# Strassen's form in the second GEMM of both FFN layers, products summed in PSUM in the first, and conditioning work moved to other stages

## The chip, the cores and the metric

One core of a Trainium2 chip runs the whole program in one launch. The metric is the device time of that launch in microseconds; the time before is the median of three runs.

## What is computed

Two layers of a diffusion backbone over 1024 latent tokens and 256 context tokens of width 1024. Layer 0 mixes by a gated convolution and differential attention, layer 1 by pooling and retention. Each layer ends in a gated ConvFFN with a hidden width of 2816, and every sub-layer is modulated by shifts, scales and gates that come from a conditioning vector. The part that matters most here:

```python
def conv_ffn(h, w_up, conv_w, conv_b, w_down):
    a, b = jnp.split(h @ w_up, 2, axis=-1)
    a = dwconv3(a, conv_w) + conv_b
    return (jax.nn.silu(a) * b) @ w_down
```

All of it is float32. The first GEMM is `h @ w_up`, the second is `(...) @ w_down`.

## The kernel before

Activations lie transposed, features on partitions and tokens in two chunks of 512 columns (chunk 0 and chunk 1). A float32 product is made of three matmuls of rounded parts: each operand is split into a high part (a ScalarE cast to fp32r) and a low part, the residual (a subtraction on VectorE or GpSimd); `mm3` (L221) adds high x high, high x low and low x high. `WStream` (L93) loads the weights in a fixed list of units on the SP queue, casts them (L111) and makes the residual (L113), a few units ahead of their use. A tile framework inserts the waits and sets each engine's order of instructions at compile time; the order is static in the program.

**First GEMM of the FFN** (`up_pair`, L867). For 20 of the 22 blocks of 128 hidden features, the pair (a, b) for both token chunks is made in a Strassen-Winograd form: 7 products of 4 x 3 matmuls (`prod`, L792), so 84 matmuls per pair. Each product has a PSUM bank of its own, eight banks in turn (seven in layer 0). The sums of products are made outside: P1 and P5 are copied by ScalarE (L887 or L884, and L894), VectorE adds P6, P2, P7, P4 and P3 (L890, L892, L897, L902, L906), and GpSimd makes two further sums (L898, L899). Then `conv_silu` (L705) does bias and middle tap on ScalarE (L708), two taps on VectorE (L709, L710) and silu on ScalarE (L712); VectorE gates the first half (L907), GpSimd the second (L908), and the block g goes to DRAM (L909). The weight sums of Strassen's form are made in `up_unit` (L771): an add on GpSimd (L783), subtractions on VectorE (L784, L788), and two of the four residuals on GpSimd. Three pairs have their first two products made in advance (`up_pre`, L858).

**Second GEMM**. Layer 0 uses `down` (L912): for each token chunk and each half of the output features, four banks are filled over 22 hidden blocks, 2 x 2 x 22 x 4 x 3 = 1056 matmuls; then VectorE adds the four banks to x (L938). Layer 1 uses `down_fast` (L968): seven products over 11 pairs of hidden blocks, four banks each, 7 x 11 x 4 x 3 = 924 matmuls, chains of products summed in PSUM without a copy, with VectorE adding to x after each of them (L1021). Loads of g and their differences are made three steps ahead.

**Conditioning of layer 1** (`mod_layer1`, L324) is 256 pieces of a matrix-vector product on VectorE (L355), each with a 128 KB load on the SP queue (L338). A row of the conditioning vector is loaded on ScalarE's queue and goes through silu there (L332, L333) whenever the half or the vector changes; one buffer holds it. 120 pieces run beside the first GEMM of layer 0, 136 beside its second GEMM. The results feed the norm ahead of layer 1 and its gates.

**Around it**. `norm` (L382) squares on ScalarE, sums on VectorE, reduces over partitions by matmuls with one column (`colsum`, L370), and spreads the result over partitions by float32 matmuls with the identity (`bcast`, L376). In layer 0 the norms for layer 1 start in the second GEMM: chunk 0 first, at steps 27 and 38, chunk 1 at the end, between the first steps of the token GEMM of layer 1 (`od_tok`, L1049), which takes the token tiles in the order 0 to 9. Behind it come feature GEMM and retention woven together (`retention`, L1227). Both stages have two banks for the GEMM's sums.

Of the kernel before, what the change touches and what calls it, by code (L numbers as in the profile page):

```python
# [9 lines left out]
F32 = mybir.dt.float32  # L10
# [38 lines left out]
XLOAD = ((2, 4, 6, 8, 25, 26, 27, 28), (1, 2, 3, 4, 6, 8, 10, 12))  # L49

DOWN = ((1, 0, 0), (5, 1, 4), (6, 1, 0), (3, 1, 0), (7, 1, 4), (2, 0, 0), (4, 0, 4))
NORM0 = 27


MODA, MODB = 120, (3, 8)
# [81 lines left out]
class Net:  # L137
# [64 lines left out]
    def _lat_units(self, units, L):  # L202
        up, dn = self.I[f"w_up{L}"], self.I[f"w_dn{L}"]
        units.extend([up[f, i] for f in range(PLAIN) for i in range(2)])
        first = range(PLAIN, PLAIN + PRE)
        units.extend([partial(self.up_unit, up, f, 0) for f in first])
        units.extend([partial(self.up_unit, up, f, i, i == 1) for f in first for i in range(1, 4)])
        units.extend([partial(self.up_unit, up, f, i) for f in range(PLAIN + PRE, NF) for i in range(4)])
        if L:
            units.extend([partial(self.down_unit, dn, p, f) for p, _, _ in DOWN for f in range(0, NF // 2, 2)])  # L210
            return
        for _ in range(2):
            for mg in range(2):
                units.extend([dn[f:f + 2, :, mg * 512:(mg + 1) * 512].rearrange("f p m -> p f m")
                              for f in range(0, NF, 2)])
# [26 lines left out]
    def mod_start(self, hp, psA, first):  # L242
# [81 lines left out]
    def mod_layer1(self, row, tile, first, last):  # L324

        nc, I = self.nc, self.I
        todo = [(v, h, mt, j) for v, n in ((1, 16), (0, 48)) for h in range(2) for mt in range(n) for j in range(2)]
# [16 lines left out]
        if last < len(todo):  # L344
            return
        for dst, n in ((self.modC, 48), (self.modD, 16)):
            for q in range(1, 4):
                nc.vector.tensor_tensor(dst[:, :, 0], dst[:, :, 0], dst[:, :, q], op=ALU.add)
            nc.vector.tensor_tensor(dst[:, :, 0], dst[:, :, 0], self.v("modb1", 0, n), op=ALU.add)
        self.gs[(1, 1, 0)] = self.gscale("n1g1", self.modC[:, 8:16, 0])  # L350
        self.gs[(1, 1, 1)] = self.gscale("n1g1", self.modD[:, 8:16, 0])
        self.gs[(1, 2, 0)] = self.gscale("n2g1", self.modC[:, 32:40, 0])
# [418 lines left out]
    def up_unit(self, up, f, i, again=False):  # L771
# [7 lines left out]
        if i == 1:  # L779
# [12 lines left out]
    def prod(self, out, W, half, B):  # L792

        for k in range(4):
            ks = slice((half * 4 + k) * P, (half * 4 + k + 1) * P)
            self.mm3(out, (W[0][:, ks], W[1][:, ks]), (B[k][:, 0, :], B[k][:, 1, :]), k == 0, k == 3)
# [70 lines left out]
    def up_pair(self, L, f, hs, T, big, ps, pre=None):  # L867
        nc = self.nc
        B11, B21, B22 = hs[0][:4], hs[0][4:], hs[1][4:]
        bank = lambda n: ps.tile([P, 512], F32, tag="mm", name=n)  # L870
# [4 lines left out]
        p1, u2, p5, u3 = t2k("p1"), t2k("u2"), u("p5"), u("u3")  # L875

        def product(n, W, half, B):
            pt = bank(n)
            self.prod(pt, W, half, B)
            return pt  # L880
# [31 lines left out]
    def down(self, xk, galloc, ps, gate, done):  # L912

        nc = self.nc
        gs = ([], [])
        loads = [(c * NF + f // 2, c, f + j) for c in range(2) for f in range(0, NF, 2) for j in range(2)]
        for c in range(2):
            for mg in range(2):
                pt = [ps.tile([P, 512], F32, tag="mm", name="pd") for _ in range(4)]
                for f in range(0, NF, 2):  # L920
                    while loads and loads[0][0] <= c * NF + mg * (NF // 2) + f // 2 + GAHEAD:
                        _, c1, j = loads.pop(0)
                        raw = self.tmp.tile([P, 512], F32, tag="t2k", name="gr")
                        nc.sync.dma_start(raw, self.gD[j][:, c1 * 512:(c1 + 1) * 512])
                        gt = galloc(j)
                        nc.scalar.copy(gt[:, 0, :], raw)
                        nc.vector.tensor_tensor(gt[:, 1, :], raw, gt.bitcast(F32)[:, 0, :], op=ALU.subtract)  # L927
                        gs[c1].append(gt)
                    W = self.ws.get()
                    for j in range(2):  # L930
                        for m in range(4):
                            ms = slice(j * 512 + m * P, j * 512 + (m + 1) * P)
                            gt = gs[c][f + j]
                            self.mm3(pt[m], (W[0][:, ms], W[1][:, ms]), (gt[:, 0, :], gt[:, 1, :]), f + j == 0, f + j == NF - 1)
                    yield
                for m in range(4):
                    mm = mg * 4 + m
                    nc.vector.scalar_tensor_tensor(xk[c](mm), in0=pt[m], scalar=gate(mm), in1=xk[c](mm),  # L938
                                                   op0=ALU.mult, op1=ALU.add)
                    done(c, mm)  # L940
# [27 lines left out]
    def down_fast(self, xk, galloc, ps, gate, done):  # L968
# [80 lines left out]
    def od_tok(self, qp, ps, hs):  # L1049
# [177 lines left out]
    def retention(self, rp, ps, feat):  # L1227
# [25 lines left out]
        for item in range(17):  # L1253
# [22 lines left out]
            fill(RFILL[2 + item])  # L1276
        for _ in range(3):
# [42 lines left out]
    def rest(self, stop=99):  # L1320
# [20 lines left out]
        def tail(L, xin, xmid, src, gate1, gs, sh, gate2, done, step=lambda phase, i, alloc: None):  # L1341

            with ExitStack() as s:
# [4 lines left out]
                ps = Pool(pF, {t: ("mm", 8) for t in ("mm", "tp", "st")} if L else {"mm": ("mm", 7), "tp": ("n", 1), "st": ("n", 1)})  # L1348
# [42 lines left out]
                s6f = lambda: s6().bitcast(F32)[:, 0, :]  # L1391
                alloc = (s6f, lambda: s6f()[:, :256])
                galloc, work = (lambda j: s4() if j < 14 else s5()), self.down
                if L:
                    self.dalloc = lambda: p4.tile([P, 1024], F32, tag="s4", name="s4f")
                    self.dS = {}
                    turn = [0]

                    def galloc():
                        turn[0] += 1  # L1400
                        return s6() if turn[0] % 3 == 0 else s5()

                    work = self.down_fast
                for i, _ in enumerate(work(xk, galloc, ps, gate2, lambda c, m: done(c, m, xk, ps))):
                    if i in XLOAD[L]:
                        next(loads[XLOAD[L].index(i) // 4])
                    step(1, i, alloc)
# [5 lines left out]
        def done0(c, m, xk, ps):  # L1413
            nc.sync.dma_start(self.xD[1][c, :, m, :], xk[c](m))
            if m == 7:
# [3 lines left out]
                next(nm[c])  # L1419
# [3 lines left out]
        def step0(phase, i, alloc):  # L1423
            if i == 0:
                mods.append(self.mod_layer1(*alloc, phase * MODA, 256 if phase else MODA))
            if phase == 0:
                pace(mods[0], i, 7 * (NF - PLAIN), MODA + 1)
            else:
                for _ in range(MODB[0] if i < NF // 2 else MODB[1]):
                    next(mods[1], None)  # L1430
            if phase == 1 and i in (NORM0, 38):
# [6 lines left out]
        with ExitStack() as s:  # L1438
            pG = s.enter_context(tc.tile_pool(name="psG", bufs=1, space=PSUM, reuse_waits="tile"))
            ps = Pool(pG, {"mm": ("mm", 2), "at": ("at", 2), "o": ("o", 2), "rst": ("rst", 2), "tp": ("rst", 2), "st": ("rst", 2)})  # L1440
            with ExitStack() as s2:
# [14 lines left out]
                for es in xs:  # L1456
                    es.close()
                next(tok)
                drain(nm[2])
                drain(tok)  # L1460
            with ExitStack() as s2:
                rp = s2.enter_context(tc.tile_pool(name="rp", bufs=1, reuse_waits="tile"))
                rr = Pool(rp, {t: (t, 2) for t in ("am", "qd", "ry", "rsq", "sg", "M", "QD", "V", "kd", "q", "St", "kT")})
                self.retention(rr, ps, self.od_feat(rp, ps, hs))
# [224 lines left out]
```

## Time and profile before

| | us |
|---|---|
| median of 3 runs (2769.24 to 2776.75) | 2772.87 |
| the profiled execution's own time | 2781.38 |
| its span, first to last instruction | 2779.6 |
| first GEMM, layer 0 / layer 1 | 409.0 / 383.5 |
| second GEMM, layer 0 / layer 1 | 286.5 / 209.5 |
| token GEMM of layer 1 | 110.5 |
| feature GEMM and retention | 185.0 |

The mean granted clock of TensorE over the span is 0.966, where 1 is 2.4 GHz and 0.5 is 1.2 GHz. The stages were cut where the tile that TensorE writes changes: P in the first GEMM, pd in the second, pt in the token GEMM, pf in the feature GEMM. In rows of groups, "x" is a number of instructions and idle time is that just before them, with what ended it. A matmul's listed duration is longer than the distance to the next one, since they overlap in the array.

### The profile page before, as it was taken

How to read it: one execution, taken by the hardware profiler on the slowest of the kernel's cores; microseconds unless marked ns; L12 is line 12 of the kernel's file. 1: busy time of each engine (PE TensorE's matmuls, PEld its weight loads, DVE VectorE, ACT ScalarE, POOL GpSimd, SP SyncE). 2: the span in 40 equal slices, each digit the busy share in tenths (PEclk: the TensorE clock that was granted, in tenths of full speed). 3: DMA queues.
4: the chain of work that ended last, by engine and by line, in shares of the span. 5: the costliest groups of instructions: out<-in, count | busy, mean ns of one | idle time of the engine just before them, and what ended most of it. 6: DMA issues, size and time to landing. Idle time of an engine off the chain costs nothing. (4 is left out here: it accounts for less than half of the span.)

```text
span 2779.6 us, 35344 instructions
## 1 busy us (share of the span) xinstructions
PE 2625.0 (94%) x12924; PEld 2206.8 (79%) x12924; DVE 1910.8 (69%) x2815; ACT 1098.5 (40%) x1635; POOL 800.5 (29%) x674
## 2 busy tenths in 40 slices
PE   7999998999898999999998989999999999999999
PEld 6877787888888787787886767787778888888887
DVE  7467856999887577777776665613356767766895
ACT  5322224666665344333333323323234333334342
POOL 3221113444342034444440000102212555544000
PEclk7999998999998999999999999999999999999999
DMA  6224625443322723333338774337363222224874
GB/s 246 93 93 144 197 96 164 127 131 109 109 89 79 245 84 121 114 124 121 123 105 272 246 224 153 121 112 223 115 235 114 76 84 90 85 91 152 286 231 165
DMA packets 203007, 402.26 MB, mean 145 GB/s; under 512 B 19536, under 2 KB 88784, under 8 KB 202448
## 3 DMA queue, kind: packets, MB, share of 16 engines
q1 hardware_dynamic: 199952, 394.87, 43.2%
q10 hardware_dynamic: 2880, 5.12, 0.6%
q8 instruction: 102, 1.67, 0.3%
q14 instruction: 73, 0.60, 0.1%
HBM read 330.19 MB, written 69.73 MB: 144 GB/s over the span
## 5 line engine op out<-in xcount | busy, mean ns | idle before, releaser
L225 PE MATMUL P<-s,wl 128*128 128x512 f32 x1120 | 440.4, 393 | 10.5 <-DVE wl L113 10.2
L223 PE MATMUL P<-s,wh 128*128 128x512 f32 x1120 | 438.9, 392 | 7.8 <-ACT p L884 4.5
L224 PE MATMUL P<-s,wh 128*128 128x512 f32 x1120 | 438.4, 391 | 0.0
L111 ACT CAST wh<-wr 128x1024 fp32r<-128x1024 f32 (+1 forms) x268 | 278.4, 1040 | 392.7 <-DMA wr<-in_w_dn 83.8
L113 DVE TENSOR_TENSOR wl<-wr,wh 128x1024 fp32r<-128x1024 f32 (+1 forms) x231 | 289.3, 1255 | 183.8 <-ACT wh L111 176.3
L223 PE MATMUL pd<-s,wh 128*128 128x512 f32 x660 | 263.2, 399 | 24.9 <-DVE x L938 16.3
L225 PE MATMUL pd<-s,wl 128*128 128x512 f32 x660 | 261.8, 397 | 2.5 <-DVE wl L113 2.5
L224 PE MATMUL pd<-s,wh 128*128 128x512 f32 x660 | 262.2, 397 | 0.6 <-DVE s L927 0.6
L225 PEld LDWEIGHTS P<-s,wl 128*128 128x128 f32 x1120 | 211.8, 189 | 59.2 <-DVE wl L113 15.5
L223 PEld LDWEIGHTS P<-s,wh 128*128 128x128 f32 x1120 | 212.1, 189 | 53.9 <-ACT p L884 5.4
L224 PEld LDWEIGHTS P<-s,wh 128*128 128x128 f32 x1120 | 211.9, 189 | 44.6
L363 POOL TENSOR_TENSOR rr<-vv,mhalf 128x8 f32<-128x8 f32 (+2 forms) x39 | 56.6, 1451 | 520.1 <-DVE vv L361 520.1
L223 PEld LDWEIGHTS pd<-s,wh 128*128 128x128 f32 x660 | 127.1, 193 | 54.3 <-DVE x L938 17.6
L225 PEld LDWEIGHTS pd<-s,wl 128*128 128x128 f32 x660 | 126.8, 192 | 30.7 <-DVE wl L113 4.1
L224 PEld LDWEIGHTS pd<-s,wh 128*128 128x128 f32 x660 | 127.1, 193 | 28.4 <-DVE s L927 1.5
L113 POOL TENSOR_TENSOR wl<-s,wh 128x1024 fp32r<-128x1024 f32 x40 | 101.6, 2540 | 148.0 <-ACT wh L111 148.0
L709 DVE SCALAR_TENSOR_TENSOR fcv<-a,vec,fcv 128x1024 f32<-128x1024 f32 (+1 forms) x66 | 71.1, 1078 | 102.6 <-ACT fcv L708 102.6
L111 ACT CAST wh<-r 128x1024 fp32r<-128x1024 f32 x80 | 67.1, 839 | 178.7 <-DVE r L784 99.7
L708 ACT ACTIVATE fcv<-a,vec 128x1024 f32<-128x1024 f32 (+1 forms) x66 | 68.5, 1037 | 174.5 <-POOL a L899 166.4
L113 POOL TENSOR_TENSOR wl<-wr,wh 128x1024 fp32r<-128x1024 f32 x37 | 94.3, 2550 | 134.0 <-ACT wh L111 125.5
L1511 ACT ACTIVATE p<-S,s 128x1280 f32<-128x1280 f32 (+1 forms) x80 | 92.6, 1158 | 69.5 <-DVE s L1509 65.4
L783 POOL TENSOR_TENSOR r<-r 128x512 f32<-128x512 f32 x40 | 72.5, 1813 | 132.1 <-DMA r<-in_w_up 100.9
(373 smaller groups left out, 6680.2 us busy)
## 6 DMA issues: line engine op xcount, KB each, us to landing
wr<-in_w_dn SPq DMA_DIRECT2D x101, 512.0 KB, 4.5
wr<-in_w_up SPq DMA_DIRECT2D x98, 512.0 KB, 3.6
gr<-gD SPq DMA_DIRECT2D x121, 256.0 KB, 4.0
gD<-fcv SPq DMA_DIRECT2D x44, 512.0 KB, 2.8
wr<-in_w_out SPq DMA_DIRECT2D x40, 512.0 KB, 3.7
r<-in_w_up SPq DMA_DIRECT2D x40, 512.0 KB, 3.3
s<-in_mod1T SPq DMA_DIRECT2D x136, 128.0 KB, 3.5
mbw<-in_mod0T SPq DMA_DIRECT2D x32, 512.0 KB, 3.9
```

The source lines that it names most:

```text
L111: self.nc.scalar.copy(hi, raw)
L113: eng.tensor_tensor(lo, raw, hi.bitcast(F32), op=ALU.subtract)
L223: mm(out, L[0], R[0], start=first, stop=False)
L224: mm(out, L[0], R[1], start=False, stop=False)
L225: self.last_mm = mm(out, L[1], R[0], start=False, stop=last)
L363: self.last_pow = nc.gpsimd.tensor_tensor(r, vv, self.mhalf[:, :n], op=ALU.pow)
L708: nc.scalar.activation(t, a[:, 1:N + 1], AF.Identity, bias=self.v(f"fcb{L}", f), scale=w[1])
L709: nc.vector.scalar_tensor_tensor(t, in0=a[:, 0:N], scalar=w[0], in1=t, op0=ALU.mult, op1=ALU.add)
L783: nc.gpsimd.tensor_tensor(r1[:, 1536:], r1[:, 512:1024], r1[:, :512], op=ALU.add)
L1511: nc.scalar.activation(e, sv, AF.Exp, bias=s2[:, m:m + 1], accum_out=self.s1[:, qt:qt + 1] if m == 0 else s2[:, 2:3])
```

## The change

- Layer 0's second GEMM takes the function of layer 1 (`down_fast`, now named `down`); the plain one goes. All eight banks serve it. Chunk 1 is done first now, so the token GEMM takes tiles 4 to 7 first, and the norm's steps are 67 and 70.
- The first GEMM of both layers sums in PSUM: P1, P6, P7 and P4 in bank A, P5 and P3 in bank B, P2 in bank C; ScalarE copies A after P1, P6 and P4 and B after P5; VectorE makes the other sums.
- GpSimd keeps no arithmetic in the first GEMM's loop: weight sum, two residuals and the second gating go to VectorE.
- Conditioning: 128 pieces beside layer 0's first GEMM, in a new order so that shift and scale are done there; the other 128 in the token GEMM (3 per step) and the retention (5 per item), with three buffers for pieces and one for the row. One buffer instead of two holds the retention's kd.
- `bcast` and the first rows use `transpose` with a broadcast operand instead of a float32 matmul.

```diff
-XLOAD = ((2, 4, 6, 8, 25, 26, 27, 28), (1, 2, 3, 4, 6, 8, 10, 12))
+XLOAD = (1, 2, 3, 4, 6, 8, 10, 12)
+NORM0 = (67, 70)
-NORM0 = 27
-MODA, MODB = 120, (3, 8)
+MODA, MODT, MODR = 128, 3, 5
...
-                    nc.tensor.matmul(rb[:, k * P:(k + 1) * P], self.silc[:, h * 4 + k, v:v + 1].broadcast_to([P, P]), self.ident,
-                                     start=True, stop=True)
+                    nc.tensor.transpose(rb[:, k * P:(k + 1) * P], self.silc[:, h * 4 + k, v:v + 1].broadcast_to([P, P]),
+                                        self.ident)
...
-        todo = [(v, h, mt, j) for v, n in ((1, 16), (0, 48)) for h in range(2) for mt in range(n) for j in range(2)]
+        todo = [(v, h, mt, j) for v, a, b in ((1, 0, 16), (0, 0, 16), (0, 16, 48)) for h in range(2) for mt in range(a, b)
+                for j in range(2)]
...
-                self.nc.tensor.matmul(rb[:, j * P:(j + 1) * P], r[:, j:j + 1].broadcast_to([P, P]), self.ident,
-                                      start=True, stop=True)
+                self.nc.tensor.transpose(rb[:, j * P:(j + 1) * P], r[:, j:j + 1].broadcast_to([P, P]), self.ident)
...
-            nc.gpsimd.tensor_tensor(r1[:, 1536:], r1[:, 512:1024], r1[:, :512], op=ALU.add)
+            nc.vector.tensor_tensor(r1[:, 1536:], r1[:, 512:1024], r1[:, :512], op=ALU.add)
...
-            return ws.split(s34, nc.gpsimd)
-        return ws.split(self.r1[:, :512], nc.gpsimd)
+            return ws.split(s34, nc.vector)
+        return ws.split(self.r1[:, :512], nc.vector)
...
         if pre:
-            nc.scalar.copy(p1, pre[0])
+            A, C = pre
+            nc.scalar.copy(p1, A)
+            yield
         else:
             W0 = self.ws.get()
-            nc.scalar.copy(p1, product("P1", W0, 0, B11))
+            A, C = (ps.tile([P, 512], F32, tag="mm", name=n) for n in ("PA", "PC"))
+            self.prod(A, W0, 0, B11)
+            nc.scalar.copy(p1, A)
+            yield
+            self.prod(C, W0, 1, B21)
+        V(p1, p1, C, op=ALU.add)
         yield
+
         W1 = self.ws.get()
-        V(u2, p1, product("P6", W1, 0, T[2]), op=ALU.add)
+        self.prod(A, W1, 0, T[2], False)
+        nc.scalar.copy(u2, A)
         yield
-        V(p1, p1, pre[1] if pre else product("P2", W0, 1, B21), op=ALU.add)
-        yield
-        nc.scalar.copy(p5, product("P5", W1, 1, T[1]))
+        B = ps.tile([P, 512], F32, tag="mm", name="PB")
+        self.prod(B, W1, 1, T[1])
+        nc.scalar.copy(p5, B)
         yield
         W2 = self.ws.get()
-        V(u3, u2, product("P7", W2, 0, T[3]), op=ALU.add)
-        nc.gpsimd.tensor_tensor(u2, u2, p5, op=ALU.add)
-        nc.gpsimd.tensor_tensor(a[:, 513:1025], u3, p5, op=ALU.add)
+        self.prod(A, W2, 0, T[3], False)
+        V(a[:, 513:1025], p5, A, op=ALU.add)
+        yield
+        self.prod(B, W2, 1, B22, False)
+        V(u2, u2, B, op=ALU.add)
         yield
         W3 = self.ws.get()
-        V(a[:, 1:513], u3, product("P4", W3, 0, T[4]), op=ALU.add)
-        yield
-        P3 = product("P3", W2, 1, B22)
+        self.prod(A, W3, 0, T[4], False)
+        nc.scalar.copy(a[:, 1:513], A)
         self.conv_silu(L, f, a, t, SEQ)
-        V(u2, u2, P3, op=ALU.add)
         V(t[:, :512], t[:, :512], p1, op=ALU.mult)
-        nc.gpsimd.tensor_tensor(t[:, 512:], t[:, 512:], u2, op=ALU.mult)
+        V(t[:, 512:], t[:, 512:], u2, op=ALU.mult)
...
-            for tt in range(10):
+            for tt in (4, 5, 6, 7, 0, 1, 2, 3, 8, 9):
...
             fill(RFILL[2 + item])
+            for _ in range(MODR):
+                next(mod, None)
+        drain(mod)
...
+                mp = s.enter_context(tc.tile_pool(name="mp", bufs=1, side="right", reuse_waits="tile"))
+                mods.append(self.mod_layer1(lambda: mp.tile([P, 512], F32, tag="cr2", name="cr2"),
+                                            lambda: mp.tile([P, 256], F32, tag="mw2", name="mw2", bufs=3), MODA, 256))
                 next(tok)
                 drain(nm[2])
-                drain(tok)
+                for _ in tok:
+                    for _ in range(MODT):
+                        next(mods[1], None)
```

## Rows read from the trace of the kernel before

**Rows 1.** The page, busy time (us, share of the span), instructions of an engine

```profile
PE 2625.0 (94%) x12924; PEld 2206.8 (79%) x12924; DVE 1910.8 (69%) x2815; ACT 1098.5 (40%) x1635; POOL 800.5 (29%) x674
```

**Rows 2.** Busy time by stage; columns in the first row; stages in order of time

```profile
core 0: us, PE busy (x) PEld busy (x) DVE busy (x) ACT busy (x) POOL busy (x), PEclk, DMA share, GB/s
1054.00:1463.00 409.00, 392.62 (x1682) 319.10 (x1680) 305.07 (x487) 140.73 (x168) 196.89 (x163) 0.98 0.37 122
1463.00:1749.50 286.50, 257.57 (x1074) 208.16 (x1073) 170.75 (x415) 93.88 (x121) 11.39 (x8) 0.94 0.70 221
1749.50:1860.00 110.50, 108.91 (x503) 89.47 (x504) 48.07 (x85) 32.13 (x55) 9.91 (x12) 1.00 0.31 105
1860.00:2045.00 185.00, 175.42 (x811) 138.47 (x810) 68.91 (x106) 57.67 (x79) 48.78 (x50) 0.96 0.53 165
2182.50:2566.00 383.50, 381.64 (x1683) 315.35 (x1682) 256.13 (x247) 144.84 (x171) 197.18 (x163) 1.00 0.29 99
2566.00:2775.50 209.50, 209.50 (x925) 173.12 (x923) 163.29 (x213) 82.09 (x114) 1.79 (x1) 1.00 0.68 229
```

**Rows 3.** The same view, instructions of tile pd alone (PE, PEld, DVE), both second GEMMs

```profile
1463.00:1749.50 286.50, 256.14 (x1056) 206.16 (x1056) 11.13 (x16) 0.94 0.70 221
2566.00:2775.50 209.50, 209.50 (x924) 173.12 (x923) 18.20 (x27) 1.00 0.68 229
```

**Rows 4.** Waits of PE in 1463 to 1750: us in total, times, longest

```profile
PE pd L223 <- DVE x L938: 16.3, 3, 7.5
```

**Rows 5.** Busy time by stage, 15 us that begin as the longest of these waits ends

```profile
1613.00:1628.00 15.00, 14.35 (x55) 11.75 (x56) 11.59 (x30) 5.32 (x8) 0.00 (x0) 0.85 0.78 260
```

**Rows 6.** Timeline of PE: start us, us, what (bcast at 2111, transposes at 1818)

```profile
2111.50 1.05 PE L379 MATMUL rb<-ident,rr 128*128 128x128 f32 x8
2112.31 0.48 PE L223 MATMUL po<-s,wh 128*128 128x512 f32 x1
...
1818.20 0.60 PE L548 MATMUL tpq<-ident,m 128*128 128x128 f32 x4
1818.56 0.48 PE L223 MATMUL pt<-wh,s 128*128 128x512 f32 x1
```

**Rows 7.** Waits of PE in 1054 to 1463, the first GEMM of layer 0

```profile
PE P L225 <- DVE wl L113: 8.6, 9, 3.5
PE P L223 <- ACT p L884: 4.3, 1, 4.3
PE P L223 <- DVE fcv L820: 2.1, 1, 2.1
```

**Rows 8.** Groups of VectorE in 2182.5 to 2566, layer 1's first GEMM: busy us, mean ns

```profile
L113 DVE TENSOR_TENSOR wl<-r,wh 128x1024 fp32r<-128x1024 f32 x20 | 44.2, 2209 | 0.0
L784 DVE TENSOR_TENSOR r<-r,wr 128x512 f32<-128x512 f32 x20 | 28.7, 1434 | 40.6 <-POOL r L783 40.6
L113 DVE TENSOR_TENSOR wl<-wr,wh 128x1024 fp32r<-128x1024 f32 x21 | 25.6, 1219 | 0.5 <-PE P L225 0.3 <-ACT wh L111 0.2
...
L902 DVE TENSOR_TENSOR a<-u,P 128x512 f32<-128x512 f32 x19 | 13.1, 689 | 15.4 <-PE P L225 14.2
```

**Rows 9.** Timeline of ACT, one turn from pair to pair, layer 1's first GEMM

```profile
2304.16 1.25 ACT L708 ACTIVATE fcv<-a,vec 128x1024 f32<-128x1024 f32 x1 [5.90 <-POOL a L899]
...
2308.55 1.06 ACT L712 ACTIVATE fcv<-fcv 128x1024 f32<-128x1024 f32 x1 [2.20 <-DVE fcv L710]
2309.52 0.57 ACT L887 COPY p<-P 128x512 f32<-128x512 f32 x1
```

**Rows 10.** Timeline of ACT, the second row of conditioning in layer 0's first GEMM

```profile
1167.82 0.34 ACTq L332 DMA_DIRECT2D cr<-in_crow  x1
1170.40 0.63 ACT L333 ACTIVATE cr<-cr 128x512 f32<-128x512 f32 x1 [6.59 <-DMA cr<-in_crow]
```

**Rows 11.** Pieces of conditioning by tile and by line L355: duration ns min/median/max

```profile
L338 SPq DMA_DIRECT2D mw<-in_mod1T x120: 327/382/1908, 1076.0 to 1461.0; - x120
...
L355 DVE SCALAR_TENSOR_TENSOR s<-s,s x136: 410/425/1520, 1475.8 to 1691.6; 128x256 f32<-128x256 f32 x136
```

More of the change, by code (lines that the diff above doesn't have):

```diff
@@ L208, in _lat_units @@
         units.extend([partial(self.up_unit, up, f, i) for f in range(PLAIN + PRE, NF) for i in range(4)])
[L209 to L215, printed above, removed]
+        units.extend([partial(self.down_unit, dn, p, f) for p, _, _ in DOWN for f in range(0, NF // 2, 2)])
     def v(self, name, i=0, n=1):
@@ L343, in mod_layer1 @@
             self.mod_piece(*d)
-        if last < len(todo):
-            return
-        for dst, n in ((self.modC, 48), (self.modD, 16)):
+        early = last == MODA
+        for dst, a, b in ((self.modC, 0, 16), (self.modD, 0, 16)) if early else ((self.modC, 16, 48),):
             for q in range(1, 4):
[L348 to L352, printed above, removed]
+                nc.vector.tensor_tensor(dst[:, a:b, 0], dst[:, a:b, 0], dst[:, a:b, q], op=ALU.add)
+            nc.vector.tensor_tensor(dst[:, a:b, 0], dst[:, a:b, 0], self.v("modb1", a, b - a), op=ALU.add)
+        if early:
+            self.gs[(1, 1, 0)] = self.gscale("n1g1", self.modC[:, 8:16, 0])
+            self.gs[(1, 1, 1)] = self.gscale("n1g1", self.modD[:, 8:16, 0])
+        else:
+            self.gs[(1, 2, 0)] = self.gscale("n2g1", self.modC[:, 32:40, 0])
     def mod_piece(self, w, c, d):
@@ L788, in up_unit, with prod @@
             nc.vector.tensor_tensor(s34, self.r0, self.r1[:, 512:1536], op=ALU.subtract)
-            return ws.split(s34, nc.gpsimd)
-        return ws.split(self.r1[:, :512], nc.gpsimd)
-    def prod(self, out, W, half, B):
+            return ws.split(s34, nc.vector)
+        return ws.split(self.r1[:, :512], nc.vector)
+    def prod(self, out, W, half, B, new=True):
         for k in range(4):
             ks = slice((half * 4 + k) * P, (half * 4 + k + 1) * P)
-            self.mm3(out, (W[0][:, ks], W[1][:, ks]), (B[k][:, 0, :], B[k][:, 1, :]), k == 0, k == 3)
+            self.mm3(out, (W[0][:, ks], W[1][:, ks]), (B[k][:, 0, :], B[k][:, 1, :]), new and k == 0, k == 3, True)
     def up_plain(self, L, hs, nm, big, ps):
@@ L869, in up_pair @@
         B11, B21, B22 = hs[0][:4], hs[0][4:], hs[1][4:]
-        bank = lambda n: ps.tile([P, 512], F32, tag="mm", name=n)
         t2k = lambda n: self.tmp.tile([P, 512], F32, tag="t2k", name=n)
@@ L874, in up_pair @@
         t = big.tile([P, SEQ], F32, tag="cv", name="fcv", bufs=2)
[L875 to L880, printed above, removed]
+        p1, u2, p5 = t2k("p1"), t2k("u2"), u("p5")
         V = nc.vector.tensor_tensor
         if pre:
-            nc.scalar.copy(p1, pre[0])
+            A, C = pre
+            nc.scalar.copy(p1, A)
+            yield
         else:
             W0 = self.ws.get()
-            nc.scalar.copy(p1, product("P1", W0, 0, B11))
+            A, C = (ps.tile([P, 512], F32, tag="mm", name=n) for n in ("PA", "PC"))
[3 more added lines that the diff above has]
+            self.prod(C, W0, 1, B21)
@@ L903, in up_pair @@
-        yield
-        P3 = product("P3", W2, 1, B22)
+        self.prod(A, W3, 0, T[4], False)
+        nc.scalar.copy(a[:, 1:513], A)
         self.conv_silu(L, f, a, t, SEQ)
-        V(u2, u2, P3, op=ALU.add)
         V(t[:, :512], t[:, :512], p1, op=ALU.mult)
-        nc.gpsimd.tensor_tensor(t[:, 512:], t[:, 512:], u2, op=ALU.mult)
+        V(t[:, 512:], t[:, 512:], u2, op=ALU.mult)
         nc.sync.dma_start(self.gD[f], t)
         yield
[L912 to L940, printed above, removed]
@@ L966, in down_unit, with down @@
         return ws.split(raw, nc.vector)
-    def down_fast(self, xk, galloc, ps, gate, done):
+    def down(self, xk, galloc, ps, gate, done):
         nc = self.nc
@@ L1225, in ret_norm, with retention @@
         nc.sync.dma_start(self.mix2[512 + h * P:512 + (h + 1) * P, c0:c0 + 512], y)
-    def retention(self, rp, ps, feat):
+    def retention(self, rp, ps, feat, mod):
         done = [0]
@@ L1347, in tail @@
                 pF = s.enter_context(tc.tile_pool(name="psF", bufs=1, space=PSUM, reuse_waits="tile"))
-                ps = Pool(pF, {t: ("mm", 8) for t in ("mm", "tp", "st")} if L else {"mm": ("mm", 7), "tp": ("n", 1), "st": ("n", 1)})
+                ps = Pool(pF, {t: ("mm", 8) for t in ("mm", "tp", "st")})
                 hs = [[], []]
@@ L1390, in tail, with galloc @@
                 loads = [load(xmid) for es, x, load in xs]
[L1391 to L1407, printed above, removed]
+                self.dalloc = lambda: p4.tile([P, 1024], F32, tag="s4", name="s4f")
+                self.dS = {}
+                turn = [0]
+                def galloc():
+                    turn[0] += 1
+                    return s6() if turn[0] % 3 == 0 else s5()
+                for i, _ in enumerate(self.down(xk, galloc, ps, gate2, lambda c, m: done(c, m, xk, ps))):
+                    if i in XLOAD:
+                        next(loads[XLOAD.index(i) // 4])
+                    step(1, i, None)
                 return [es for es, x, load in xs]
@@ L1418, in done0 @@
                                     late=True))
-                next(nm[c])
+                next(nm[-1])
         mods = []
         def step0(phase, i, alloc):
-            if i == 0:
-                mods.append(self.mod_layer1(*alloc, phase * MODA, 256 if phase else MODA))
             if phase == 0:
+                if i == 0:
+                    mods.append(self.mod_layer1(*alloc, 0, MODA))
                 pace(mods[0], i, 7 * (NF - PLAIN), MODA + 1)
[L1428 to L1431, printed above, removed]
+            if phase == 1 and i in NORM0:
                 next(nm[0])
```

4 lines of the change are left out of this document (2 added, 2 removed).

## The prediction, made before the changed kernel ran

> **What bounds the kernel now.** I read the page first: TensorE is busy for 94% of the span [rows 1]. That share says little about what is lost, so I next read a table by stage [rows 2], whose stretches I set where the tile that TensorE writes changes. It holds each second GEMM and each first GEMM twice, once per layer, and they run differently. In layer 1 TensorE has no gap: its Strassen second GEMM is 209.5 us for 924 matmuls at clock 1.00 [rows 2, 3], so one 512-column matmul costs 209.5/924 = 0.2267 us; its first GEMM is 383.5 us for 20 x 84 = 1680 matmuls, which at that pitch are 380.9. In layer 0 the plain second GEMM takes 286.5 us for 1056 matmuls [rows 2, 3], which would be 239.4 at that pitch; 47 us are lost, 28.9 of them idle (286.5 less 257.6 busy), most of the rest by a mean clock of 0.94. The waits name what TensorE stood for above all: VectorE's read-out of four sums before their banks could be used again (seven banks, two sets of four) [rows 4]. From the end of the longest gap, 7.5 us, the granted clock averages 0.85 over 15 us [rows 5]: part of them ran at 1.2 GHz and the rest at 2.4, which is 0.15 x 15 = 2.3 us of work lost on top of the gap. The first GEMM of layer 0 takes 409 us for the same 1680 matmuls, 28 us over the pitch.
>
> So TensorE is the bound, and what counts is its number of matmuls and the waits that reach it.
>
> **The sum** is made against the profiled execution: span 2779.6, its time 2781.4, which is 8.5 above the median of 2772.9. I carry the difference over to the median.
>
> *Second GEMM of layer 0.* 1056 matmuls become 7 x 11 x 12 = 924. Layer 1 shows this very code at 209.5 us, with all its loads (DMA share 0.68), VectorE at 163 us and no wait. Layer 0 adds the norm of chunk 1 inside the stage: eight one-column and four transposing matmuls, about 1.5 us of TensorE by the row of eight at 0.81 (2111.50 to 2112.31) [rows 6], and on VectorE 7 or 8 sums, 8 scalings and 4 residuals of 512 columns, 20 x 0.69 = 14 us [rows 8], which makes 177 of some 213. The squares share four tmp buffers with the loads of g, so I allow 2.5 us. 209.5 + 1.5 + 2.5 = 213.5, a gain of **73**. Ends: no allowance, 75; two waits like the three of [rows 4], at 5.4 each and 2.3 for the clock, 58. The 136 modulation pieces leave this stage, which frees VectorE of 136 x 0.5 us [rows 11].
>
> *Transposes.* A 128-column bcast by float32 matmul is two records 0.1 us apart: eight take 0.81 [rows 6]. Four transposes take 0.36 before the next matmul starts (1818.20 to 1818.56). Counted in the code, bcast makes 110 column blocks in a run and the first rows 16, so 126 records go, at (0.81 - 0.36)/4 = 0.112: 14 us. Some stand next to a wait. I take **12**; ends 0 (a broadcast operand transposed at the old price) and 14.
>
> *First GEMM, the engines.* VectorE has 256 us in layer 1 [rows 2], 12.8 per pair of 19.1. It gains an add of 512 (0.69), the residual of S34 (1.22), that of the last half (0.69), the second gating (0.69), and loses two PSUM sums net of the one that replaces GpSimd's (2 x 0.69): +1.9. But its operations beside a running GpSimd shrink to what they cost without: the residual 2.21 to 1.22, the subtraction 1.43 to 0.69 [rows 8]: -1.7. Equal. ScalarE gains two copies of 0.57 [rows 9] to the 144.84/20 = 7.2 per pair [rows 2]. Both stay under TensorE's 19.1 and are costed at nothing on average; if TensorE's cover went, 1 us per pair would show.
>
> *First GEMM, the order.* Here a wait is added. Today every product has a bank of its own. Now P1, P6, P7 and P4 go into one bank A, which must be read after each; between two of them stands one other product, 12 x 0.2267 = 2.72 us of cover (P2, P5, P3), and P5 and P3 share bank B likewise. Queued behind a held P6 are all of TensorE's later matmuls. A copy of 0.58 fits easily unless ScalarE is held. ScalarE's queue shows how it can be: the copy of p1 comes behind the previous pair's silu, which waits for VectorE's two taps [rows 9]. From the end of P4: copy 0.57; from the start of the bias to the end of silu 5.45 (2304.16 to 2309.61), less 0.69 for the sum of P3, which stands between the taps today and comes earlier then; copy of p1 0.57. That is 5.9, against P1 + P2 = 5.44. So 0.5 us per pair if the order stays, 1.15 if another operation stands between the taps, nothing if the copy goes first. I take 0.4 for 37 of the 40 pairs (the three at layer 0's start stand in waits already): **+15**, ends 0 and 43.
>
> *First GEMM of layer 0 otherwise.* Of its 28 us of loss, VectorE's late weight residuals are 8.6 and the start 4.3 + 2.1 [rows 7], with the clock behind them. GpSimd's slow links leave that chain, which helps. Against this stand the rows of conditioning: 128 pieces need four, not three, and a row holds ScalarE for 6.6 us (wait for the buffer, then the load) [rows 10]; with copies that TensorE now awaits, that is 6.6 + 0.6 - 2.7 = 4.5 us, with the clock some 6.5, for three rows 20, and 8 for the start. I take **0**; ends -28 and +10.
>
> *The moved pieces.* 128 of 256 go to the token GEMM (3 per step) and the retention (5 per item). Each is a load on SP (0.38 us to issue, 3 buffers, held until an earlier piece is done, with weight and store issues queued behind it) and 0.5 us on VectorE [rows 11]: 64 us of VectorE in 295 us where it is busy for 117 [rows 2]. Hidden by the matmuls there. Two rows hold ScalarE 6.6 us each against 24 x 0.2267 = 5.4 us of cover by two banks. **+6**, ends 0 and 25.
>
> Four small edits (token order, norm steps, x loads, one buffer for kd, whose reader is done two items before the next load) cost nothing: the matmuls of four token steps, 22 us, cover the late chunk's norm as today.
>
> -73 - 12 + 15 + 0 + 6 = **-64**: 2772.9 - 64 = 2709.
>
> **Rivals.**
> A. *Bank A becomes the bound* (slower). If two of the four windows of a pair are missed, by 1.2 us each plus 0.2 of clock, that is 2.6 x 37 = 96 against 79 won elsewhere: 2790. It decides from 2.1 us per pair. For it: static order [rows 9], waits for VectorE's read-out today [rows 4]. Against: cover 2.7, copies 0.6, ScalarE and VectorE both idle for a third or more. The Trainium skill, PSUM — Partial Sum Buffer, section on PSUM bank collisions, says that the hardware neither arbitrates nor stalls two engines on one bank, so software must keep them apart. By it a product never overlaps the copy of its own bank, as I assumed; the waits for x in layer 0 agree, at 16.3 us.
> B. *The first GEMMs clear altogether*: layer 0 falls to the pitch (-28) and no window is missed (-15): 2666. For it: layer 1 at 383.5 today; against: the rows' waits.
> C. *The waits come back in the second GEMM*: norm, loads and 28 read-outs (16 now) cost it what the old waits did, and only 132 x 0.2267 = 30 and 12 are won, less 21: 2752. Against: layer 1's stretch.
>
> That the change doesn't do what it says is small here: the matmul count is in the code.
>
> **How the numbers follow.** Forecast 0.62, B 0.15, C 0.15, A 0.08. The range reaches to B on one side and to C on the other, 2672 to 2750, leaving A and the outer halves of B and C out. A measurement can tell some 0.3%, 8 us: faster 0.88, same 0.05 (between C and A), slower 0.07.
>
> **What would show it.** The second GEMM of layer 0 at 210 to 220 us with 924 matmuls and clock 0.99 or more; a transpose row of 38 x 1 for rb instead of 76; POOL near nothing in the first GEMMs and the residual there at 1.22; waits of P for p, u, a under 1 us each; token and retention stretches within 10 us of 110.5 and 185. Wrong would be: P waiting for ScalarE's copies in every pair, clock under 0.97 in layer 1's first GEMM, or a second GEMM of over 230.

## The result

The changed kernel takes 2704.78 us, the median of four runs (2699.01 to 2705.93), beside 2773.8 for the kernel before: a ratio of 0.9753, interval 0.9736 to 0.977. The forecast was 2709. By stage, from the first instruction of a stage to the first of the next (us, one profiled execution each; the execution of before that was profiled is some 8 us above its median):

| stage | before | after | forecast of the change |
|---|---|---|---|
| up to layer 0's out projection | 916.3 | 906.5 | part of -12 |
| first GEMM, layer 0 | 412.3 | 398.7 | 0 (order: +7 of +15) |
| second GEMM, layer 0 | 282.9 | 222.7 | -73 |
| token GEMM to the end of layer 1's out projection | 384.8 | 392.7 | +6 |
| first GEMM, layer 1 | 383.3 | 385.9 | +8 of +15 |
| all others | 400.0 | 397.6 | |
| span | 2779.6 | 2704.1 | -64 |

Two things matter for reading the table. The forecast counted layer 0's second GEMM from the last matmul of the first (286.5 us, and 409.0 for the first); by that cut the change is 286.5 to 223.0 and 409.0 to 398.7. And a stage differs by some us between profiled executions of the same code: the old second GEMM took 282.9 us here and 276.5 in the kernel of before with transposes alone; the first GEMM of layer 0 in its new form took 392.6 to 398.7 in the five traces that have it.

The page's busy line and the table of busy time by stage of the changed kernel, with the columns of [rows 2]; the stages are first and second GEMM of layer 0, token GEMM, features with retention, first and second GEMM of layer 1:

```profile
PE 2564.4 (95%) x12666; PEld 2153.4 (80%) x12666; DVE 1971.4 (73%) x3010; ACT 1164.4 (43%) x1749; POOL 425.7 (16%) x434
```

```profile
1044.00:1442.70 398.70, 385.79 (x1681) 316.33 (x1681) 301.32 (x556) 173.59 (x216) 10.36 (x46) 0.99 0.43 141
1442.70:1665.70 223.00, 215.28 (x939) 175.93 (x937) 182.80 (x239) 102.25 (x146) 7.72 (x5) 0.98 0.69 230
1665.70:1785.40 119.70, 115.75 (x530) 95.09 (x531) 69.53 (x184) 34.70 (x58) 9.99 (x12) 1.00 0.49 158
1785.40:1961.00 175.60, 164.47 (x737) 126.52 (x736) 98.28 (x257) 56.02 (x75) 48.19 (x49) 0.95 0.76 225
2104.80:2490.60 385.80, 382.62 (x1681) 316.32 (x1680) 253.28 (x289) 167.75 (x209) 10.48 (x46) 1.00 0.29 100
2490.60:2700.00 209.40, 209.40 (x926) 173.29 (x924) 162.00 (x212) 82.87 (x116) 0.00 (x0) 1.00 0.68 227
```

GpSimd is near nothing in the first GEMMs, and VectorE's time there did not rise: 253 us in layer 1 where it was 256 [rows 2]. What TensorE waited for, first in layer 0's second GEMM, then in its first (us in total, times, longest):

```profile
PE pd L219 <- ACT s L967: 4.9, 1, 4.9
PE pd L220 <- DVE s L968: 2.0, 3, 1.4
...
PE P L219 <- ACT u L889: 5.4, 1, 5.4
PE PA L219 <- DVE a L897: 3.6, 4, 1.5
PE P L219 <- ACT p L875: 2.1, 1, 2.1
PE PB L219 <- ACT p L893: 1.2, 1, 1.2
```

The waits for the read-out of x [rows 4] are gone. New is one wait of 4.9 us for the cast of a block of g. SyncE's timeline ahead of it shows why: a step of 2.7 us needs one more block of g, but for 8 us SyncE issues nothing. Its next load of g waits that long for the norm of chunk 1 (L416), which holds the tmp buffers:

```profile
1638.24 0.33 SPq L107 DMA_DIRECT2D wr<-in_w_tok  x1
1646.80 1.65 SPq L948 DMA_DIRECT2D gr<-gD  x2
```

```profile
SPq L948 <- DVE s L416: 8.2, 1, 8.2
```

VectorE's groups in layer 1's first GEMM (busy us, mean ns) against [rows 8], and ScalarE's turn from pair to pair against [rows 9]:

```profile
L115 DVE TENSOR_TENSOR wl<-r,wh 128x1024 fp32r<-128x1024 f32 x20 | 24.4, 1219 | 0.0
...
L781 DVE TENSOR_TENSOR r<-r,wr 128x512 f32<-128x512 f32 x20 | 13.7, 686 | 0.1
...
L897 DVE TENSOR_TENSOR a<-p,PA 128x512 f32<-128x512 f32 x17 | 11.7, 690 | 12.1 <-PE PA L221 12.1
```

```profile
2301.22 0.58 ACT L904 COPY a<-PA 128x512 f32<-128x512 f32 x1
2301.84 1.25 ACT L705 ACTIVATE fcv<-a,vec 128x1024 f32<-128x1024 f32 x1
2303.22 0.59 ACT L881 COPY p<-PA 128x512 f32<-128x512 f32 x1
...
2306.67 1.05 ACT L709 ACTIVATE fcv<-fcv 128x1024 f32<-128x1024 f32 x1
```

The residual fell from 2.21 to 1.22 us and the subtraction from 1.43 to 0.69. And the static order is another one than before: the copy of p1 now comes ahead of silu, and TensorE waits for no bank in layer 1's running pairs; its only wait there is at the start:

```profile
PE P L219 <- ACT u L889: 3.2, 1, 3.2
```

### The profile page after: what moved, and what is told of

It reads as the page before. It is cut to its first block, busy times and chain, and to the rows that moved or that the text cites. A ratio compares the mean times of both kernels' runs of the same rounds, so it can differ in the third digit from the quotient of the medians.

```text
span 2704.1 us, 34748 instructions
## 1 busy us (share of the span) xinstructions
PE 2564.4 (95%) x12666; PEld 2153.4 (80%) x12666; DVE 1971.4 (73%) x3010; ACT 1164.4 (43%) x1749; POOL 425.7 (16%) x434
## 4 chain that ended last, share of the span: by engine, by line
PE 51%; DVE 14%; issue 12%; DMA 7%; ACT 2%; POOL 2%; SPq 0%; ACTq 0%; DVEq 0%; POOLq 0%
PE PA L219 4%; PE PA L220 4%; PE PA L221 4%; PE pd L220 3%; PE pd L221 3%; PE pd L219 3%; PE PB L220 2%; PE PB L221 2%; PE PB L219 2%; PE po L220 2%; PE po L221 2%; PE po L219 2%; DVE wl L115 2%; DMA mw<-in_mod1T 1%; DMA r<-in_w_up 1%
## 5 line engine op out<-in xcount | busy, mean ns | idle before, releaser
L113 ACT CAST wh<-wr 128x1024 fp32r<-128x1024 f32 x254 | 262.0, 1033 | 411.5 <-PE PA L220 69.6
L219 PE MATMUL pd<-s,wh 128*128 128x512 f32 x616 | 240.8, 391 | 4.9 <-ACT s L967 4.9
L220 PE MATMUL pd<-s,wh 128*128 128x512 f32 x616 | 241.1, 391 | 2.0 <-DVE s L968 2.0
L219 PE MATMUL PA<-s,wh 128*128 128x512 f32 x544 | 212.1, 390 | 3.6 <-DVE a L897 3.6
L221 PE MATMUL PA<-s,wl 128*128 128x512 f32 x544 | 211.7, 389 | 0.0
L220 PE MATMUL PA<-s,wh 128*128 128x512 f32 x544 | 211.6, 389 | 0.0
L353 DVE SCALAR_TENSOR_TENSOR mw<-mw,cr 128x256 f32<-128x256 f32 x256 | 111.9, 459 | 82.6 <-DMA mw<-in_mod1T 73.6
L219 PEld LDWEIGHTS pd<-s,wh 128*128 128x128 f32 x616 | 116.0, 188 | 29.7 <-ACT s L967 5.8
L220 PEld LDWEIGHTS pd<-s,wh 128*128 128x128 f32 x616 | 116.2, 189 | 27.7 <-DVE s L968 3.6
L219 PE MATMUL PB<-s,wh 128*128 128x512 f32 x320 | 124.6, 389 | 1.2 <-ACT p L893 1.2
L220 PE MATMUL PB<-s,wh 128*128 128x512 f32 x320 | 124.5, 389 | 0.0
L221 PE MATMUL PB<-s,wl 128*128 128x512 f32 x320 | 124.5, 389 | 0.0
L219 PEld LDWEIGHTS PA<-s,wh 128*128 128x128 f32 x544 | 102.1, 188 | 26.5 <-DVE a L897 5.3
L221 PEld LDWEIGHTS PA<-s,wl 128*128 128x128 f32 x544 | 102.1, 188 | 21.2
L220 PEld LDWEIGHTS PA<-s,wh 128*128 128x128 f32 x544 | 102.1, 188 | 21.0
```

The source lines that it names most:

```text
L113: self.nc.scalar.copy(hi, raw)
L219: mm(out, L[0], R[0], start=first, stop=False)
L220: mm(out, L[0], R[1], start=False, stop=False)
L221: self.last_mm = mm(out, L[1], R[0], start=False, stop=last)
L353: self.nc.vector.scalar_tensor_tensor(w, in0=w, scalar=1.0, in1=c, op0=ALU.mult, op1=ALU.mult, accum_out=d)
```

## The experiments

Twelve kernels ran. Unless it says otherwise each is the changed kernel with one edit, and a difference in us is that of the ratios to before times 2774.

**Transposes alone**, on the kernel before.

```diff
-self.nc.tensor.matmul(rb[:, j * P:(j + 1) * P], r[:, j:j + 1].broadcast_to([P, P]), self.ident, start=True, stop=True)
+self.nc.tensor.transpose(rb[:, j * P:(j + 1) * P], r[:, j:j + 1].broadcast_to([P, P]), self.ident)
...
```

(The first rows of conditioning are changed likewise.)

> The kernel before with only the transposes in place of the float32 bcast matmuls. Theory (TensorE-bound, 126 records of 0.112 us fall away): 8 to 14 us faster than before, most of it ahead of 917 us where 80 + 36 of the records stand. Rival (the attention stage is bound by ScalarE and VectorE, so TensorE's time there is free): 0 to 3 us. A second rival, that a broadcast operand is transposed at the matmul's price: 0, with four transposes at 0.8 us.

Ratio 0.9989, interval 0.9977 to 1.0001: 3 us, 6 at most, so the rival's end. The price of one is as forecast; the changed kernel's timeline of TensorE has four in 0.35 us, against eight records in 0.81 [rows 6]:

```profile
2036.26 0.60 PE L377 MATMUL rb<-ident,rr 128*128 128x128 f32 x4
2036.61 0.48 PE L219 MATMUL po<-s,wh 128*128 128x512 f32 x1
```

Its profiled execution is shorter ahead of 917 us (901.1), as is that of every kernel with transposes (901 to 909, against 916.3 and 914.0 for two without), but the runs don't confirm a gain of that size. Why the freed time is mostly not won was not followed up.

**The plain second GEMM** in layer 0, with eight banks and without pieces beside it.

```diff
+                work = self.down
+                if L == 0:
+                    galloc, work = (lambda j: s4() if j < 14 else s5()), self.down_plain
...
```

(With it the old token order, norm steps 27 and 38 and loads of x come back.)

> The changed kernel, but layer 0's second GEMM is the plain one of before, with eight banks and no modulation pieces beside it. Theory (the matmul count gives 30 us and the old waits came from seven banks and the pieces): the stage takes 245 to 255 us against 222.7, the run 22 to 32 us longer than the changed kernel. Rival (the plain order of four banks filled and read out together stalls by itself): the stage stays at 275 to 285, the run 50 to 62 us longer.

Ratio 0.9798 (0.9778 to 0.9818), 12 us longer than the changed kernel. Its second GEMM of layer 0 by busy time:

```profile
1435.60:1676.40 240.80, 240.80 (x1070) 199.52 (x1069) 111.70 (x127) 89.32 (x115) 8.44 (x5) 1.00 0.51 167
```

1056 matmuls at the pitch, with not one gap: better than the theory. So of the 60 us that this stage lost in the change, 42 come without Strassen's form (36, if the 276.5 of the run above is taken as the old stage), and the form adds 18 of the 30 that its 132 fewer matmuls are worth. By the runs' times it adds 12, with some 5 us of uncertainty on each of the two.

**Eight banks on the kernel before**, pieces left where they were.

```diff
-ps = Pool(pF, {t: ("mm", 8) for t in ("mm", "tp", "st")} if L else {"mm": ("mm", 7), "tp": ("n", 1), "st": ("n", 1)})
+ps = Pool(pF, {t: ("mm", 8) for t in ("mm", "tp", "st")})
```

> The kernel before with eight banks in layer 0 instead of seven and one for the norm; the pieces stay beside its second GEMM. If the seven banks made the waits for VectorE's read-out: second GEMM of layer 0 from 282.9 to 255 to 262 us, run 15 to 28 us shorter than before. If the 136 pieces on VectorE made them (in the plain variant of the changed kernel both were gone): the stage stays at 275 to 285 and the run within 6 us of before.

Ratio 0.9965 (0.9952 to 0.9979), 10 us; the stage takes 272.1, between the two, but only 4 us under the 276.5 of the run with transposes alone. The largest wait of TensorE in its second GEMM, and below it that in the run with transposes alone, which has seven banks:

```profile
PE pd L223 <- ACT s L926: 19.8, 2, 16.0
```

```profile
PE pd L223 <- DVE x L937: 18.2, 3, 7.5
```

What held SyncE's queue here around the wait of 16 us (1595 to 1630):

```profile
SPq L338 <- DVE s L355: 17.4, 15, 3.3
```

The seven banks did make the read-out waits: all three are gone. A single wait of 16 us for g took their place: the loads of pieces wait in SyncE's queue for VectorE's pieces, with the loads of g behind them. The squares of the norm share the tmp buffers with g here too; but the plain second GEMM above, with the same norm steps and no pieces, has no such wait. So eight banks alone don't clear the stage, and eight banks without pieces do (240.8). Seven banks without pieces were not run.

**The first GEMM of before.**

```diff
-        self.prod(A, W1, 0, T[2], False)
-        nc.scalar.copy(u2, A)
+        V(u2, p1, product("P6", W1, 0, T[2]), op=ALU.add)
...
-            return ws.split(s34, nc.vector)
+            return ws.split(s34, nc.gpsimd)
```

> The changed kernel with the first GEMM of before: a bank for every product, sums on VectorE and GpSimd, weight work on GpSimd. Theory (the 13.7 us won in layer 0's first GEMM come from taking GpSimd out of the chain): layer 0's stage back at 408 to 414 us, layer 1's at 383, the run 8 to 14 us longer than the changed kernel. Rival (they come from the eighth bank and from where the pieces lie): layer 0's stage at 396 to 401 and the run unchanged or 2 us shorter.

Ratio 0.9912 (0.9896 to 0.9929), 44 us longer, far more than the theory's 8 to 14: 32 us in layer 0's first GEMM and 8 in the second behind it (231.2). Layer 0's stage by busy time, and its largest wait:

```profile
1042.00:1472.80 430.80, 398.18 (x1682) 322.99 (x1680) 308.13 (x508) 144.16 (x173) 195.76 (x163) 0.96 0.37 124
```

```profile
PE P L221 <- DVE wl L115: 22.1, 11, 4.6
```

It needs 18 us more than in the kernel before, beside 128 pieces and four rows instead of 120 and three. Layer 1, which has no pieces, is unmoved at 383.6. The eighth bank is not the cause, as the run above has 412.0 with it. Which of the pieces, the fourth row and their new order costs the old form these 18 us was not run apart; the new form stands beside the same pieces without the loss.

**GpSimd for the weights alone**, products summed in PSUM.

```diff
-            nc.vector.tensor_tensor(r1[:, 1536:], r1[:, 512:1024], r1[:, :512], op=ALU.add)
+            nc.gpsimd.tensor_tensor(r1[:, 1536:], r1[:, 512:1024], r1[:, :512], op=ALU.add)
...
-        return ws.split(self.r1[:, :512], nc.vector)
+        return ws.split(self.r1[:, :512], nc.gpsimd)
```

> The changed kernel, with products summed in PSUM, but the weight add and two residuals on GpSimd as before. Theory (GpSimd in the chain of the weights is what holds layer 0's first GEMM): that stage at 412 to 431 us against 398.7, the run 12 to 30 us longer than the changed kernel, layer 1's stage within 3 of 385.9. Rival (the sums in PSUM bring it): stage at 402 or less.

Ratio 0.9782 (0.9764 to 0.9799), 8 us longer; layer 0's stage 404.4, between the two expectations. GpSimd's weight work costs 6 to 12 us there, against the five traces of the new form. Layer 1's first GEMM, with VectorE's residual and subtraction in it:

```profile
2106.60:2493.80 387.20, 383.41 (x1681) 316.24 (x1680) 204.22 (x227) 167.21 (x210) 108.70 (x105) 1.00 0.28 99
```

```profile
L115 DVE TENSOR_TENSOR wl<-r,wh 128x1024 fp32r<-128x1024 f32 x20 | 24.4, 1219 | 0.0
...
L781 DVE TENSOR_TENSOR r<-r,wr 128x512 f32<-128x512 f32 x20 | 13.9, 693 | 40.2 <-POOL r L780 40.2
```

GpSimd works for 109 us here, and yet both have the short times, 1.22 and 0.69 us; of the forty, one alone meets an instruction of GpSimd. So it is not GpSimd's work as such that lengthens them, but two instructions at the same time, as in the kernel before, where this residual began just behind one of GpSimd's and ended 1.1 us after it:

```profile
2333.95 2.41 POOL L113 TENSOR_TENSOR wl<-s,wh 128x1024 fp32r<-128x1024 f32 x1 [3.53 <-ACT wh L111]
2334.01 3.43 DVE L113 TENSOR_TENSOR wl<-r,wh 128x1024 fp32r<-128x1024 f32 x1
```

From here, moving the three operations to VectorE costs it 49 us (204 to 253), about their full price.

**A bank for each product, GpSimd out**, all sums on VectorE.

```diff
-        nc.gpsimd.tensor_tensor(u2, u2, p5, op=ALU.add)
-        nc.gpsimd.tensor_tensor(a[:, 513:1025], u3, p5, op=ALU.add)
+        V(u2, u2, p5, op=ALU.add)
+        V(a[:, 513:1025], u3, p5, op=ALU.add)
```

(The diff is against the kernel before; the rest of `up_pair` is as there, with the last gating on VectorE too.)

> The changed kernel with GpSimd out of the first GEMM, but a bank for every product and all sums on VectorE. Theory (GpSimd out of the chain is enough): layer 0's stage at 394 to 402 us, layer 1's at 383 to 387, the run within 5 us of the changed kernel. Rival (the sums in PSUM bring it, as VectorE has two 512-column operations more per pair): layer 0's stage at 410 or more.

Ratio 0.9715 (0.9699 to 0.9732), 11 us shorter than the changed kernel. First GEMMs of layer 0 and 1:

```profile
1043.60:1430.10 386.50, 382.96 (x1681) 316.52 (x1680) 338.67 (x629) 146.82 (x175) 11.70 (x44) 1.00 0.42 140
...
2101.80:2482.60 380.80, 380.80 (x1682) 315.45 (x1681) 301.86 (x367) 146.67 (x171) 10.42 (x44) 1.00 0.29 100
```

VectorE carries 37 to 49 us more per layer, and yet TensorE loses nothing in layer 1. From 430.8 to 386.5 in layer 0, with only GpSimd's operations moved: that is where the old loss was. Summing in PSUM is no help to time. Between these two traces it costs 12 and 5 us; over all traces of either form (five and three, us) some 8 and 3, which is the 11 us of the runs:

| first GEMM | summed in PSUM | a bank for each product |
|---|---|---|
| layer 0 | 398.7, 392.6, 394.3, 396.1, 395.4 | 386.5, 388.0, 387.4 |
| layer 1 | 385.8, 382.7, 385.7, 384.5, 383.3 | 380.8, 381.2, 381.4 |

**Copies made three times**, to delay the release of banks A and B by 1.16 us.

```diff
-        nc.scalar.copy(u2, A)
+        [nc.scalar.copy(u2, A) for _ in range(3)]
...
```

(The copies of p1 and p5 likewise.)

> The changed kernel with the copies of p1, u2 and p5 out of banks A and B made three times each, which delays the release of the bank by 1.16 us. Theory (a product of 2.7 us covers 0.2 + 3 x 0.58 = 1.9 us): layer 1's first GEMM stays within 385 to 392 us, and the waits of PA and PB for ScalarE stay under 10 us there. Rival A of the prediction (any late copy is a stall, with the clock behind it): 20 pairs x 1 to 2 us, 405 or more.

Ratio 0.978 (0.9765 to 0.9794), 7 us longer. Layer 1's first GEMM, the only wait of TensorE's matmuls that its trace lists there, which stands at the start, and the largest wait of its weight loads (PEld):

```profile
2106.80:2499.40 392.60, 388.01 (x1681) 315.70 (x1681) 252.13 (x287) 237.72 (x330) 10.42 (x46) 0.99 0.28 98
```

```profile
PE P L219 <- ACT u L889: 4.6, 1, 4.6
```

```profile
PEld PB L219 <- ACT p L893: 6.4, 19, 0.4
```

Twenty pairs with 70 us more on ScalarE (238 against 168). Bank A is in time, but bank B is late in 19 pairs of 20: the first weight load of its next product waits for the third copy of p5, 0.3 us each. 392.6 lies at the theory's upper end, 7 above the changed kernel. Of this 1.4 is the longer wait at the start and some 2 a lower clock behind it (0.94 against 0.97 over the first 55 us). The rest is bank B: in 330 us of running pairs, both without a gap and at clock 1.00, there are 18 matmuls fewer than in the changed kernel, which are 4 us at the pitch. First the two stretches of this run, then those of the changed kernel:

```profile
2106.80:2162.00 55.20, 50.61 (x211) 41.13 (x211) 38.48 (x43) 31.59 (x47) 8.03 (x10) 0.94 0.33 113
2160.00:2490.00 330.00, 330.00 (x1440) 268.66 (x1440) 210.02 (x240) 202.20 (x278) 2.39 (x36) 1.00 0.26 90
```

```profile
2104.80:2160.00 55.20, 52.02 (x223) 42.59 (x222) 42.20 (x47) 25.85 (x35) 8.23 (x12) 0.97 0.35 119
2158.00:2488.00 330.00, 330.00 (x1458) 273.21 (x1457) 210.53 (x243) 142.12 (x176) 2.38 (x36) 1.00 0.27 95
```

The theory's 1.9 us left out the cast that stands ahead of the copies in ScalarE's queue:

```profile
2317.80 1.05 ACT L113 CAST wh<-s 128x1024 fp32r<-128x1024 f32 x1 [0.66 <-PE PB L220]
2318.75 1.82 ACT L893 COPY p<-PB 128x512 f32<-128x512 f32 x3
```

The late bank costs some 0.2 us per pair, far from rival A's 1 to 2.

**A longer lead for g.**

```diff
-GAHEAD = 3
+GAHEAD = 6
```

> The changed kernel with the loads of g made six steps ahead instead of three. Theory (the 4.9 us gap in layer 0's second GEMM comes because the norm of chunk 1 holds the tmp buffers for some 10 us, which three steps of 2.7 don't cover): the gap goes, the stage falls from 222.7 to 211 to 216, the run 5 to 10 us shorter. Rival (a load still waits for one of four tmp buffers, so a longer lead is never built up): stage within 3 of 222.7.

Ratio 0.9712 (0.9697 to 0.9726), 11 us shorter, 8 of them in this stage. The gap of 4.9 us is gone:

```profile
1437.40:1652.20 214.80, 212.28 (x938) 174.28 (x937) 182.37 (x239) 102.60 (x146) 7.58 (x5) 1.00 0.71 236
```

**Without the late pieces.** The 128 pieces moved behind the second GEMM are left out, and gates and shifts that they give are zero.

```diff
+        if last > MODA:
+            nc.vector.memset(self.modC[:, 16:48, :], 0.0)
+            todo = []
```

> The changed kernel without the 128 pieces that were moved into the token GEMM and the retention: their loads, products and rows are left out and the gates they would give are zero. Theory (the pieces delay the end of the retention and the loads behind it): token GEMM to the start of the first GEMM's plain part falls from 392.7 us by about 8 to the 384.8 of before. Rival (hidden; the longer stages have another cause, the new order of the tokens or the single kd buffer): under 2 us.

Ratio 0.9702 (0.9683 to 0.9721), 14 us shorter. From the token GEMM to the plain part of the first GEMM it takes 385.5, against 392.8 by the same view of the changed kernel: 7 us. Every trace with these pieces has 390.5 us or more there, every one without them 386.2 or less. The other half of the 14 lies in stages whose work is the same, by less than such stages differ between traces, and stays open.

**Pieces earlier.**

```diff
-MODA, MODT, MODR = 128, 3, 5
+MODA, MODT, MODR = 128, 4, 7
```

> The changed kernel with the moved pieces set denser: four per token step and seven per retention item, so that they are done before the last items. Theory (the pieces that run into the end of the retention delay the last items and the loads behind them): token GEMM to the plain part of the first GEMM falls from 392.7 to 385 to 389 us. Rival (their price is spread, or denser pieces only hold VectorE's and SP's queues earlier): within 3 of 392.7 or longer.

Ratio 0.976 (0.9735 to 0.9784), and the stretch takes 394.5. The rival holds: the price is not one of the last items. Whether it is spread over the stretch or denser pieces only hold the queues earlier, the run doesn't tell.

**Two and three edits together**: the `up_pair` with own banks and the longer lead, then the earlier pieces too.

```diff
-        nc.gpsimd.tensor_tensor(u2, u2, p5, op=ALU.add)
+        V(u2, u2, p5, op=ALU.add)
...
-GAHEAD = 3
+GAHEAD = 6
...
-MODA, MODT, MODR = 128, 3, 5
+MODA, MODT, MODR = 128, 4, 7
```

(The last edit in the second of them only.)

> The changed kernel with both edits that won alone: a bank for every product with all sums on VectorE, and six steps of lead for g. Theory (the two act in different stages and add): layer 0's first GEMM 384 to 392 us, its second 211 to 218, the run some 2686 to 2692 where before is 2775, ratio 0.967 to 0.970. Rival (they share tmp buffers and VectorE, one takes back the other): no shorter than 0.971.

> All three edits on the changed kernel. Theory: as the run with two edits, less 3 to 6 us, ratio to before 0.965 to 0.968. Rival: the same as with two, or longer by what the token GEMM loses.

Both are at 0.9694 (0.9673 to 0.9715, and 0.967 to 0.9718). The run with two edits lies within its theory: 16 us better than the changed kernel, where 11 and 11 were won apart. With some 5 us of uncertainty on each, it is open whether they add in full. The third edit wins nothing on top, as its rival says. With 2687.01 us the first of them beats both kernels; first and second GEMM of layer 0 there:

```profile
1048.80:1436.80 388.00, 382.98 (x1681) 316.49 (x1681) 339.98 (x629) 146.87 (x175) 10.26 (x45) 1.00 0.42 139
1436.80:1654.80 218.00, 213.33 (x938) 175.44 (x936) 184.99 (x244) 104.01 (x147) 7.58 (x5) 0.99 0.72 241
```

## Why the prediction was right, and where its terms were off

The forecast was -64 and the runs show -69, so direction and size held, and no rival came true. The terms were less good than their sum. Of the signs named, the count of matmuls, the rows of transposes, GpSimd near nothing, the residual at 1.22 and the token and retention stretches came; the second GEMM at 210 to 220 with clock 0.99 (223.0, 0.98) and waits under 1 us in the first GEMMs (5.4, 3.6, 3.2) did not.

- *Second GEMM, -73.* Measured -63.5 by the forecast's cut. The stage takes 223 instead of 213.5: the 2.5 us allowed for squares and loads sharing four tmp buffers was the right place and too little. It cost one wait of 4.9, a second of 1.4, and the clock; a longer lead for g brings the stage to 214.8. The step was sound in saying that a wait would sit there. What it did not say is how little of the 73 is Strassen's: the plain form, rid of its waits, would have had 36 to 42.
- *The cause of the old waits.* Seven banks were named. That is a part: with eight banks and the pieces still there, a 16 us wait for g came instead. The pieces were credited only with freeing VectorE; that their loads held SyncE's queue was missed.
- *Transposes, -12.* The price per record was right, and the runs give 3 us, 6 at most: the sum took most of TensorE's freed time as won, and it was not.
- *Engines, 0.* Right: 253 us on VectorE against 256. The Trainium skill, GPSIMD Engine Reference, section Specifications, has GpSimd's SBUF interfaces shared with VectorE, in contention with VectorE instructions that have two SBUF inputs. The trace agrees: those fell to 1.22 and 0.69 us without GpSimd, and the sum with one operand in PSUM kept its 0.69. They fall as far where GpSimd still works, but not at the same time (GpSimd for the weights alone).
- *Order of the banks, +15.* Its size is close: own banks save 11 us, some 8 and 3 by stage. That is luck, as the mechanism was not the one named. The order changed at compile time, so silu does not hold the copy; what remains are the start of each layer (5.4 and 3.2) and, beside pieces, VectorE's sum into a, 3.6. Rival A fell with the tripled copies: a bank that is late in nearly every pair, by 0.3 us, costs 0.2 us per pair at a clock of 1.00. The cover of 2.7 us is enough for one copy, not for three behind a cast.
- *First GEMM of layer 0 otherwise, 0.* The mis-sized step. -13.6 came out with the banks' cost in it (-10.3 by the forecast's cut); with a bank for each product it is -24 to -26 (386.5 to 388.0 against 412.3). I priced three rows at 6.5 us, because copies would wait behind ScalarE's load; no wait for ScalarE is listed in the running pairs beyond 1.2 us. And taking GpSimd out of the stage was worth far more than I gave it: 430.8 to 386.5 beside 128 pieces.
- *Pieces, +6.* Measured +8 in the stretch, where leaving them out gives back 7.

So the sum came right because errors cancelled, which is luck: some 10 us too much for the second GEMM and 9 for the transposes, against 17 too little for layer 0's first GEMM (+7 forecast with its share of the order, -10.3 measured) and 5 for layer 1's (+8, +2.6).

## What to carry to other kernels

Before a GEMM is replaced by one with fewer matmuls, clear the waits of the plain one and see what is left: here more came from an eighth bank and from loads that no longer queued in front of others than from the 132 matmuls. An engine at 29% can be the slow link of a chain; moving its work to one at 69% made that one no busier in the first GEMMs, and the chain shorter. Where products are summed in place, count what stands between two of them, and look at the order that was compiled, not at the one that was.

## What was not expected of the hardware

VectorE's operations on two SBUF tensors lasted on average up to twice as long beside GpSimd (1.43 against 0.69 us, 2.21 against 1.22), and single ones nearly three times (3.43) where both worked at once. So moving four of GpSimd's operations per pair to VectorE, with two sums less there, left VectorE's busy time where it was. A float32 transpose of a broadcast column costs 0.09 us in a dense stream, against 0.20 for the same spread by a float32 matmul, and that difference was hardly seen in the run's time.
